# One group for linear attention's outputs, rests of x last, small products padded, a shorter Newton step: a hybrid decoder layer

## The chip, the cores and the metric

The kernel runs on one core of a Trainium2 chip. The metric is the device time of one execution in microseconds (us), median over several runs. A profile of one execution stands beside it, with its own time.

The core has five engines, each with its own queue of instructions: TensorE (PE; PEld is its load of the stationary operand), VectorE (DVE), ScalarE (ACT), GpSimd (POOL) and SyncE (SP), which here issues nearly all DMAs. An engine takes its instructions in the order in which they were written for it, and waits by semaphores.

## The reference, cut to what matters

One decoder layer for 512 prompt tokens and 8 running sequences of one new token each. One projection of x (1024 wide) gives the columns of two mixers and their gates:

```python
h = jnp.einsum('btd,de->bte', x, w_in)
qa, ka, va, za, ga, qb, kb, vb, gb = jnp.split(h, split_points, axis=-1)
log_a = log_sigmoid(einsum(za, w_alpha2) + b_alpha) / 16
o_a, s_new = gla_chunked(qa, ka, va, log_a, s0, chunk)      # gated linear attention, 4 heads
o_a = o_a * lax.rsqrt(jnp.mean(jnp.square(o_a), -1, keepdims=True) + RMS_EPS) * gla_norm_g
o_b = dilated_attention(qb, k_all, v_all, q_idx, rel_bias)  # 8 heads, three window patterns
mix = jnp.concatenate([o_a * silu(ga), o_b * silu(gb)], axis=-1)
y = jnp.einsum('bte,ed->btd', mix, w_out)
x_new = layer_norm(DEEPNORM_ALPHA * x + y, ln_g, ln_b)
```

In a chunk of linear attention an output is the product of the chunk's own attention matrix with the values, plus the product of the decayed queries with the state before the chunk. For the running sequences the 1024 past keys and values are read from a cache.

## The kernel before, in words

**A planner writes the order.** Every step is a generator (`dense`, `gla_out`, `sample_softmax`, ...) that yields one operation at a time, or waits for a mark (`At`), a buffer (`Need`), several at once (`Pair`) or a batch that stays together (`Batch`). `Plan.run` (L300) takes, again and again, the operation that can start soonest by estimated costs (L95 to L123), ties by the step's priority, and writes it to its engine. So all five queues are fixed when the program is built, from estimates, and another cost or another buffer can move operations on any engine. All operations are written at L359; a reader finds them by the names of their tiles. Among the estimates is one for a change of TensorE's tile form: `SWITCH = 230.0` ns.

**Buffers** are slots by tag (L58): among them `t2=3`, `pr=4`, `t1=6`, `sv=4`. PSUM has eight banks: three `d`, three `s`, two `t`.

**Products in full precision.** A float32 operand is split in a high part, cut by ScalarE's copy to a shorter format, and a rest, which VectorE subtracts (`split`, L412). A product is three: high x high, high x rest, rest x high. Weights (hi, lo) and x (xh, xl) both go that way. Other small products are taken in plain float32, which the trace shows as two passes each.

**The stages.** `first_loads` (L536) loads x in eight slices of 128 features and the weights of ka in between, `zw`, the constants `cf` and the table `rel_bias`, copied to 64 rows (`rb_raw`, L554, two DMAs); then `weight_loads` runs through the other weight groups, two raw buffers at a time. `first_splits` (L563) splits x slice by slice, the first slice in two column ranges (`TS`: the 256 first tokens with the 8 samples, and the 256 last), the others whole, and marks `xs` each. `dense` (L681) starts with warm-up products, then takes ka: for each slice k and column range u, for both halves i of ka's features, the three products in a row (L691 to L696). It waits for x's rest before any of a slice's products. Then come za, qa, qb, kb, vb, gb, va and ga, and the output projection: `out_first` (L1473) takes the features of tokens 0 to 255 and the samples, `out_unit` (L1461) the last 256 tokens.

**Linear attention** (`gla_levels`, `gla_diagonal`, `gla_state`, `gla_queries`) builds the attention matrices `att0`, `att1`, the states `st_all` after each of four token tiles, and the decayed queries. `gla_out(u)` (L961) then takes the outputs of two token tiles: a batch of 8 products att x values with 128 rows and of 4 or 8 products queries x state with 64 rows each, into two `s` banks. It is started twice, u = 0 after the first state, u = 1 after the third. `gla_head` (L981) evacuates them and normalises; `mix_a` (L1393) multiplies with the gate.

**The running sequences.** `sample_queries` (L1211) loads for each of them the keys (`past`) and its query, copied to all partitions (`qbc`, a `t2` buffer); GpSimd multiplies, VectorE adds up into `lt`. `sample_softmax` (L1231) sums in one bank, `ps_sl`, a table product (66 rows, 64 columns), the new key's logits (32 rows, 64 columns) and the transposed `lt` (128 rows, 64 columns); softmax, `psd_s` to DRAM, and a product `ps_pn` with 64 rows. `sample_values`, `sample_gla` follow; `mix_sample_a` and `mix_sample_b` make their part of the output projection's input.

**The ends.** `residual_sample` (L1525) normalises the samples' output on 64 rows, with two sums over features by products of 64 rows and 64 columns (`ps_ms`, `ps_vs`). `norm(t)` (L1560) normalises a token tile: `rsqrt` (L388) with `between` set takes the logarithm, the exponential and then a Newton step on ScalarE in four instructions (square, times x, times -0.5 plus 1.5, times the estimate), while VectorE centres the tile; then VectorE scales and adds, and the tile is stored.

## Time and profile before

| | |
|---|---|
| median of 3 runs | 287.93 us (287.79 to 289.35) |
| the profiled execution, its own time | 288.67 us |
| its span | 286.8 us |
| instructions | 6896 |
| TensorE's clock as granted, mean | 0.994 |
| HBM read, written | 45.17 MB, 6.03 MB |

The span runs from the first instruction of the program to the last; the execution's own time holds a little more around it. Busy shares of the engines are averages over stages that differ, so a part of the change is read in its own stage. In a row of the timeline the columns are the start in us, the time that the row's instructions span, engine, line, operation, output tile and its inputs, TensorE's tile form (rows * columns) where it has one, shape, count, and in brackets the idle time before it with what ended it. Matmuls overlap: the distance from one start to the next is what a product costs, not its own duration.

### The profile page before, as it was taken

The numbers are of one execution on the slowest core, as the hardware profiler recorded it, in microseconds if no ns is written. First come the engines' busy times: TensorE is split into PE (matmuls) and PEld (weight loads), VectorE is DVE, ScalarE is ACT, GpSimd is POOL, SyncE is SP. The second block draws the span as 40 slices with busy tenths as digits, with TensorE's granted clock in tenths as the row PEclk, the third lists the DMA queues.
The fourth block names the chain that finished last, engine by engine and source line by source line (L and its number), as shares of the span: only waits on it lengthen the run. The fifth ranks groups of instructions, "written<-read, shape, count | busy, mean of one in ns | idle before, by whom it ended". The sixth has DMA issues, their size and how long they took to land.

```text
span 286.8 us, 6896 instructions
## 1 busy us (share of the span) xinstructions
PE 275.0 (96%) x2636; PEld 259.5 (90%) x2636; DVE 225.7 (79%) x547; ACT 167.5 (58%) x478; POOL 55.9 (19%) x74
## 2 busy tenths in 40 slices
PE   8999999999999998999999999999999999999990
PEld 5899999998989998899989999999999999997880
DVE  3846897999889968988889997864888995339745
ACT  5757664554567777566869867526689774113201
POOL 4000001000782444401604444540000000000000
PEclk9999999999999999999999999999999999999997
DMA  7966522225866797648998987559754788741211
GB/s 209 269 191 195 147 75 75 75 78 167 296 201 222 196 287 230 175 130 243 274 201 188 239 227 219 149 149 228 221 95 148 230 297 252 111 151 73 78 75 73
DMA packets 58936, 51.18 MB, mean 178 GB/s; under 512 B 12555, under 2 KB 50197, under 8 KB 58903
## 3 DMA queue, kind: packets, MB, share of 16 engines
q1 hardware_dynamic: 58794, 50.66, 63.2%
q8 instruction: 21, 0.34, 0.5%
q14 instruction: 13, 0.10, 0.1%
q10 hardware_dynamic: 108, 0.07, 0.1%
HBM read 45.17 MB, written 6.03 MB: 179 GB/s over the span
## 4 chain that ended last, share of the span: by engine, by line
PE 71%; DVE 13%; DMA 8%; ACT 5%; issue 2%; SPq 1%; DVEq 0%; ACTq 0%
PE ps_qb L359 8%; PE ps_yf L359 8%; PE ps_y L359 8%; PE ps_ga L359 6%; PE ps_kb L359 4%; PE ps_qa L359 4%; PE ps_gb L359 4%; PE ps_va L359 4%; PE ps_ka L359 4%; DMA raw_gb__2152<-in_w_in_dram 3%; DMA out_dram<-feat 3%; PE ps_pt L359 2%; PE ps_va_f L359 2%; PE ps_l L359 2%; PE ps_s L359 2%; PE ps_pv L359 2%
## 5 line engine op out<-in xcount | busy, mean ns | idle before, releaser
L359 POOL TENSOR_TENSOR vv<-vv,pb 128x256 f32<-128x256 f32 x32 | 26.1, 846 | 45.5 <-DMA pb<-psd_s 39.8
L359 POOL TENSOR_TENSOR past<-past,qbc 128x256 f32<-128x256 f32 x32 | 25.6, 831 | 43.4 <-DMA past<-in_ck_dram 36.0
L359 ACT ACTIVATE pr<-pr,ms 128x128 f32<-128x128 f32 (+3 forms) x49 | 26.1, 546 | 5.8 <-DVE ms L359 5.2
L359 PE MATMUL ps_pt<-cf,pr 128*128 128x128 f32 x80 | 14.1, 280 | 1.4 <-DVE pt L359 1.0
L359 DVE CUSTOM_DVE_ANT_0 pr<-ps_s,strip 128x128 f32<-128x128 f32 (+3 forms) x32 | 14.3, 476 | 0.0
L359 PE MATMUL ps_ka<-xx,hi_ka 128*128 128x264 f32 (+1 forms) x64 | 13.5, 307 | 0.3 <-DVE xx L359 0.3
L359 ACT ACTIVATE sg<-sg 128x264 f32<-128x264 f32 (+1 forms) x32 | 13.4, 419 | 0.2
L359 PEld LDWEIGHTS ps_ka<-xx,hi_ka 128*128 128x128 f32 x64 | 11.0, 205 | 1.2 <-DVE xx L359 0.8
L359 DVE TENSOR_TENSOR ptl<-ps_pt,pth 128x384 fp32r<-128x384 f32 (+1 forms) x16 | 9.8, 617 | 2.8 <-ACT pth L359 2.8
L359 PEld LDWEIGHTS ps_pt<-cf,pr 128*128 128x128 f32 x80 | 9.0, 140 | 3.3 <-DVE pt L359 1.6
L359 ACT ACTIVATE d<-d 128x512 f32<-128x512 f32 x13 | 7.8, 637 | 6.7 <-DVE d L359 6.7
L359 ACT COPY feat_y<-ps_yf 128x256 f32<-128x256 f32 x8 | 3.0, 371 | 12.7 <-PE ps_yf L359 12.7
L359 ACT ACTIVATE rstd<-mv 128x1 f32<-128x1 f32 x4 | 0.7, 199 | 15.9 <-DVE mv L359 15.9
L359 POOL MEMSET att<- 64x512 f32 x2 | 1.0, 523 | 44.5 <-DVE ks L359 44.5
L359 ACT CAST pth<-ps_pt 128x384 fp32r<-128x384 f32 (+1 forms) x16 | 8.4, 534 | 2.2 <-PE ps_pt L359 2.0
L359 DVE TENSOR_REDUCE o_pv<-vv 128x4 f32<-128x1024 f32 x8 | 9.7, 1212 | 0.0
L359 DVE TENSOR_REDUCE lt<-past 128x16 f32<-128x1024 f32 x8 | 9.6, 1199 | 0.0
L359 PE MATMUL ps_ka<-xx,lo_ka 128*128 128x264 f32 (+1 forms) x32 | 9.4, 295 | 0.0
L359 DVE TENSOR_TENSOR obT<-ps_pv,pvl 64x256 f32<-64x256 f32 x16 | 6.6, 415 | 3.5 <-ACT pvl L359 3.3
L359 DVE TENSOR_TENSOR xx<-x_raw,xx 128x520 fp32r<-128x520 f32 (+2 forms) x9 | 5.8, 640 | 4.6 <-ACT xx L359 4.6
L359 ACT COPY pvl<-ps_pv 64x256 f32<-64x256 f32 x16 | 5.5, 370 | 6.1 <-PE ps_pv L359 5.3
L359 DVE TENSOR_TENSOR d<-b 128x1024 f32<-128x1024 f32 x7 | 8.5, 1218 | 0.0
(535 smaller groups left out, 1092.4 us busy)
## 6 DMA issues: line engine op xcount, KB each, us to landing
past<-in_ck_dram SPq DMA_DIRECT2D x8, 512.0 KB
vv<-in_cv_dram SPq DMA_DIRECT2D x8, 512.0 KB
pb<-psd_s SPq DMA_DIRECT2D x16, 256.0 KB
qbc<-qsd SPq DMA_DIRECT2D x8, 256.0 KB
strip<-tabr SPq DMA_DIRECT2D x8, 256.0 KB
y<-in_xp_dram SPq DMA_DIRECT2D x4, 512.0 KB
x_raw<-in_xT_dram SPq DMA_DIRECT2D x7, 260.0 KB
out_dram<-y SPq DMA_DIRECT2D x3, 512.0 KB
```

What stands on the lines that cost most here:

```text
L359: getattr(eng.eng, op.fn)(*op.args, **op.kw)
```

## The change

It has four parts.

1. `gla_out` runs once, for all four token tiles: four banks from `s` and `t` together, 16 products att x values, then the 12 with the states. It waits for the third state.
2. In ka's products a slice's four products with x's high part go first, the two with x's rest last. Slices 1 and 2 are split in the two column ranges as well, as slice 0 was.
3. Products with fewer than 128 rows or columns are padded to full size: those of `ps_sl`, `ps_pn`, `ps_ms` and `ps_vs`. The table is loaded twice as wide, the constants `sel` and `avg` on 128 rows; `l32`, `pn_r` and `sums` are cleared first; `lt` gets a third part, where `q_s` and `k_s` now lie. The raw copy of the second table (`cts_raw`) takes a `t2` buffer instead of a `pr` one.
4. In `rsqrt` with `between`, the variance is made -0.5 (x + eps), the logarithm takes it times -2, and one instruction does what "times x" and "times -0.5 plus 1.5" did.

```diff
+N_HALF = 3
...
         if between:
 
+            yield V.tensor_scalar(x, x, eps, -0.5, op0=ALU.add, op1=ALU.mult)
+            yield S.activation(o, x, AF.Ln, scale=-2.0)
+            yield S.activation(o, o, AF.Exp, scale=-0.5)
             add(between, 5)
             yield S.activation(t, o, AF.Square)
-            yield S.mul(t, t, x)
-            yield S.activation(t, t, AF.Copy, scale=-0.5, bias=1.5)
+            yield S.activation(t, t, AF.Copy, scale=x, bias=1.5)
             yield S.mul(o, o, t)
...
-        B["rb_raw"] = yield Need("t1", "rb_raw", [64, NB, HB])
+        B["rb_raw"] = yield Need("t1", "rb_raw", [64, 2 * NB, HB])
...
-                yield from split(xraw[a // 2][:, a % 2, c], xh[a][:, c], xl[a][:, c])
-                mark("xs")
+                for c in (c,) if b or a >= N_HALF else TS:
+                    yield from split(xraw[a // 2][:, a % 2, c], xh[a][:, c], xl[a][:, c])
+                    mark("xs")
...
-                for i in range(2):
-                    yield from three(pk[i, u][:, :TW[u]], k, halves(k, u, groups[f"ka{i}"]))
+                for last in (False, True):
+                    for i in range(2):
+                        pairs = halves(k, u, groups[f"ka{i}"])
+                        for j in (1,) if last else (0, 2):
+                            yield T.matmul(pk[i, u][:, :TW[u]], *pairs[j], start=k == 0 and j == 0, stop=k == KT - 1 and last)
...
-    def gla_out(u):
+    def gla_out():
 
-        yield At("st", 2 * u + 1)
+        yield At("st", 3)
...
-        ps = yield Pair(*(bank("s", f"ps_oa{u}{h2}") for h2 in range(2)))
+        banks = yield Pair(*(bank(("s", "t"), f"ps_oa{u}{h2}") for u in range(2) for h2 in range(2)))
...
-        sel = yield Need("t1", "sel", [64, C_AV - C_E2])
-        yield D.dma_start(sel, c_f[:64, C_E2:C_AV])
+        sel = yield Need("t1", "sel", [P, C_AV - C_E2])
+        yield D.dma_start(sel, c_f[:, C_E2:C_AV])
...
-        raw = yield Need("pr", "cts_raw", [66, T_W - T_D])
+        raw = yield Need("t2", "cts_raw", [66, T_W - T_D])
...
-        yield T.matmul(ps[:64, :258], rb.rearrange("p b h -> p (b h)"), cts, start=True, stop=False, skip_group_check=True)
-        yield T.matmul(ps[:64, 256:257], l32, one[:32], start=False, stop=False, skip_group_check=True)
+        yield T.matmul(ps[:, :258], rb.rearrange("p b h -> p (b h)"), cts, start=True, stop=False, skip_group_check=True)
+        yield T.matmul(ps[:, 256:257], l32, one, start=False, stop=False, skip_group_check=True)
         for k in range(2):
-            yield T.matmul(ps[:64, k * P:k * P + P], lt[:, k, :], ident, start=False, stop=k == 1, skip_group_check=True)
+            yield T.matmul(ps[:, k * P:k * P + P], lt[:, k:k + 2, :].rearrange("p a b -> p (a b)"), ident, start=False, stop=k == 1, skip_group_check=True)
...
-        yield T.matmul(ps[:64, 0:1], avg, sums[:, 0:1], start=True, stop=True)
+        yield T.matmul(ps[:, 0:1], avg, sums[:, 0:1], start=True, stop=True)
```

More of the change, by code (lines that the diff above doesn't have):

```diff
@@ L921, in gla_state @@
         st = B["st"] = yield Need("g", "st_all", [P, TT, 2, P])
-        plan.share(st, 3)
+        plan.share(st, 2)
         kv = yield Pair(*(bank("s", f"ps_kv{cc}") for cc in range(2)))
@@ L971, in gla_out @@
                         B["st"][h2 * 64:h2 * 64 + 64, 2 * u + j - 1, m, :], start=False, stop=j + m == 2, skip_group_check=True)
-               for j in range(2) for m in range(2) for h2 in range(2) if u + j]
+               for u in range(2) for j in range(2) for m in range(2) for h2 in range(2) if u + j]
         yield mm
         free(qd, B["st"], *att)
-        plan.share(va, 2)
-        for h2 in range(2):
-            plan.share(ps[h2], 2)
-        for j in range(2):
-            add(gla_head(u, j, ps, po), 26 + u + j / 2)
+        for u in range(2):
+            plan.share(B[f"va{u}"], 2)
+            ps = banks[2 * u:2 * u + 2]
+            for h2 in range(2):
+                plan.share(ps[h2], 2)
+            for j in range(2):
+                add(gla_head(u, j, ps, {k[1:]: x for k, x in po.items() if k[0] == u}), 26 + u + j / 2)
```

69 lines of the change are left out of this document (36 added, 33 removed).

## The prediction

> **What bounds the kernel now.** I read the page's engine totals first, then the busy time by stage, then TensorE's timeline where the change edits it. Every instruction sits on helper line L359, so rows are found by tile.
>
> ```profile
> PE 275.0 (96%) x2636; PEld 259.5 (90%) x2636; DVE 225.7 (79%) x547; ACT 167.5 (58%) x478; POOL 55.9 (19%) x74
> ...
> 8.00:18.00 10.00, 10.00 (x82) 9.79 (x82) 6.53 (x12) 6.14 (x10) 0.00 (x0) 1.00 0.97 272
> ...
> 112.00:124.00 12.00, 10.65 (x83) 9.18 (x82) 11.69 (x30) 8.33 (x24) 6.01 (x7) 1.00 0.56 165
> ...
> 268.00:279.30 11.30, 11.27 (x73) 10.02 (x71) 6.63 (x12) 1.40 (x6) 0.00 (x0) 1.00 0.13 51
> ```
>
> The columns of a stage are its length, then busy time of TensorE, its weight loads, VectorE, ScalarE, GpSimd, the granted clock, the DMA share and GB/s. TensorE is busy 275.0 of 286.80 us, and full in the last product stage. What it no longer has to do, or no longer waits for, comes off the end unless something later holds it. The stage from 112 to 124 us is the exception: TensorE is busy 10.65 of 12.00 and VectorE 11.69, so there VectorE sets the pace. The 82 products from 8 to 18 us give 10.00/82 = 0.12 us per product.
>
> The profiled execution took 288.67 us, its span 286.80, so 1.87 us lie around the span. The median of the three runs is 287.93 (287.79 to 289.35), 0.74 below the profiled one. I sum the terms against 288.67 and subtract the sum from the median.
>
> **First products.** In each of the eight slices of x a product takes the high part, and another the rest, which ScalarE and then VectorE must make first.
>
> ```profile
> 6.39 0.62 ACT L359 CAST xx<-x_raw 128x520 fp32r<-128x520 f32 x1 [0.76 <-DMA x_raw<-in_xT_dram]
> 7.05 0.70 DVE L359 TENSOR_TENSOR xx<-x_raw,xx 128x520 fp32r<-128x520 f32 x1 [0.96 <-ACT xx L359]
> ...
> 7.07 0.39 PE L359 MATMUL ps_ka<-xx,hi_ka 128*128 128x264 f32 x1
> 7.80 0.39 PE L359 MATMUL ps_ka<-xx,hi_ka 128*128 128x264 f32 x1 [0.34 <-DVE xx L359]
> ...
> 9.52 0.19 PEld L359 LDWEIGHTS ps_ka<-xx,hi_ka 128*128 128x128 f32 x1 [0.21 <-DVE xx L359]
> ```
>
> The second slice's first product starts at 7.07, its second at 7.80, after the rest ends at 7.75: 0.73 less one pitch of 0.12 is 0.61 us lost. The third slice loses 0.21. After the change four products go ahead of the two that take the rest, so the rest is needed at 7.07 + 4 x 0.12 = 7.55. Halves cost at least half and at most all of a whole: the first half's rest is ready between 6.39 + 0.31 + 0.35 = 7.05 and 6.39 + 0.62 + 0.70 = 7.71. I take it as ready. TensorE then ends the first products 0.61 + 0.21 = 0.82 us sooner at best, and 0.66 if the half costs all of a whole.
>
> But that is not yet time won. The next group's weights come through a queue that the change lengthens:
>
> ```profile
> 236.08 13.93 SPq L359 DMA_DIRECT2D out_dram<-kw  x16
> ...
> 10.03 1.65 SPq L359 DMA_DIRECT2D rb_raw<-in_rel_bias_dram  x2
> ...
> 13.27 0.38 SPq L359 DMA_DIRECT2D raw_qa__174<-in_w_in_dram  x1
> ...
> 17.11 1.05 ACT L359 CAST hi_qa__264<-raw_qa__174 128x1024 fp32r<-128x1024 f32 x1 [1.81 <-DMA raw_qa__174<-in_w_in_dram]
> ...
> 18.27 1.15 DVE L359 TENSOR_TENSOR lo_qa__265<-raw_qa__174,hi_qa__264 128x1024 fp32r<-128x1024 f32 x1
> ...
> 20.44 0.41 PE L359 MATMUL ps_qa<-xx,hi_qa__264 128*128 128x264 f32 x2
> ```
>
> The two rb_raw transfers go from 256 pieces each to 512, and SyncE already spends 1.65 us on issuing them, ahead of raw_qa. ScalarE waits 1.81 us for raw_qa, so a later issue moves hi_qa and lo_qa. With 0.82 us gained TensorE reaches qa at 19.62 and wants lo_qa two products later, at 19.86; lo_qa ends at 18.27 + 1.15 = 19.42. The cover is 0.44 us. The issue grows by nothing up to all of 1.65: at that end lo_qa ends at 21.07, where before it was wanted at 20.68, and 0.39 is lost. The nearest row is the keys' store, whose 16 transfers also have 512 pieces each (32 rows of 16) and take 13.93/16 = 0.87 us: two are 1.74, 0.09 more than now, which the cover takes. If the cover is gone, each further us of issue costs one. I take the middle of 0.66 and 0.82, so 0.74 us gained, bounds -0.39 to 0.82. The extra instructions of the halves on ScalarE and VectorE are in the 0.66.
>
> **One output group.** Two groups run, each 16 passes of full size and then passes on 64 rows.
>
> ```profile
> 200.82 1.95 PE L359 MATMUL ps_oa<-va,att 128*128 128x128 f32 x16
> ...
> 202.69 0.71 PE L359 MATMUL ps_oa<-st_all,qa 64*128 64x128 f32 x8
> 203.34 0.39 PE L359 MATMUL ps_ga<-xx,lo_ga__2975 128*128 128x264 f32 x1
> ...
> 206.07 1.95 PE L359 MATMUL ps_oa<-va,att 128*128 128x128 f32 x16
> ...
> 207.95 1.16 PE L359 MATMUL ps_oa<-st_all,qa 64*128 64x128 f32 x16
> ...
> 209.04 0.51 PE L359 MATMUL ps_ga<-xx,hi_ga__2974 128*128 128x256 f32 x2
> ```
>
> Eight 64-row passes more take (209.04 - 207.95) - (203.34 - 202.69) = 0.44 us, so eight cost 0.44 and leaving costs 0.65 - 0.44 = 0.21. Entering costs 1.87 less 16 passes at 0.11 (0.44/4 for a pair is the same pitch), 0.11. One of two entries and exits falls away: 0.32, and the first product after the exit, which is slow too, gives up to another 0.12. I take 0.40, bounds 0.32 to 0.44. The price is that the first group's results come with the second's, and four of the five s and t banks are held. The group waits for the last state; gate products, which lie behind no wait of it, fill TensorE until then, as they did between 203.34 and 206.07.
>
> **Padded products.** Products on 64 rows or columns become full size.
>
> ```profile
> 259.66 0.39 PE L359 MATMUL ps_y<-lo_wo__3465,mha 128*128 128x512 f32 x1
> 259.98 0.27 PE L359 MATMUL ps_ms<-sums_s,avg 64*64 64x1 f32 x2
> 260.18 0.50 PE L359 MATMUL ps_y<-hi_wo__3464,mla 128*128 128x512 f32 x1
> 260.52 0.40 PE L359 MATMUL ps_y<-hi_wo__3525,mha 128*128 128x512 f32 x1
> ...
> 247.42 0.38 PE L359 MATMUL ps_yt<-cf,feat_y 128*128 128x128 f32 x2
> 247.56 0.37 PE L359 MATMUL ps_yf<-mhb,lo_wo__3690 128*128 128x264 f32 x1
> 247.76 0.28 PE L359 MATMUL ps_yf<-mlb,hi_wo__3689 128*128 128x264 f32 x1
> ...
> 123.47 0.28 PE L359 MATMUL ps_sl<-cts,rb 66*64 66x258 f32 x1
> 123.68 0.27 PE L359 MATMUL ps_sl<-cf,l 32*64 32x1 f32 x2
> 123.88 0.65 PE L359 MATMUL ps_sl<-cf,lt 128*64 128x128 f32 x4
> 124.46 0.50 PE L359 MATMUL ps_pv<-pt,vhl 128*128 128x256 f32 x2
> ```
>
> From 259.66 to 260.52 TensorE does two 512-wide products and the two passes of ps_ms in 0.86 us. Two such products take about 4 x 0.12 = 0.48 (a 512-wide one moves twice a 256-wide one's columns), so ps_ms costs 0.38. The nearest full-size row is ps_yt: two passes begin at 247.42, and the second product after them at 247.76, 0.34 less one product's 0.12: 0.22. Each of the two sums saves 0.16, both 0.32 (bounds 0 to 0.5). The logits take 124.46 - 123.47 = 0.99 now; full size they are one product at 0.12 and six passes at 0.11, 0.78. That saves 0.21, bounds 0 to 0.33. The small product ps_pn follows score products in their own 64-row form now and so pays no entry of its own; padded it costs up to 0.22: I take 0.09 lost.
>
> The Trainium skill, TensorEngine Tiling (Array Packing), section Performance Considerations, speaks against this: a contraction of at most 64 rows should use row tiling. By it the sum would be 0.44 smaller. The 16 row-tiled passes of ps_oa here agree, running eight in 0.44 us, but ps_ms has no partner to share the array with.
>
> The padding adds clears on VectorE: 128x128, 128x32 and 128x2.
>
> ```profile
> 18.17 0.17 DVE L359 MEMSET tsb<- 8x128 f32 x1
> ```
>
> In the stage paced by VectorE the first costs about this, 0.17; the others are covered (VectorE has 12.00 - 11.69 = 0.31 us idle in that stage). Without cover the three cost 0.51.
>
> **Newton step.** Only the last token tile's is on the path.
>
> ```profile
> 281.41 0.29 ACT L359 ACTIVATE newton<-newton,mv 128x1 f32<-128x1 f32 x1
> 281.74 0.20 ACT L359 ACTIVATE newton<-newton 128x1 f32<-128x1 f32 x1
> 281.97 0.29 ACT L359 ACTIVATE rstd<-rstd,newton 128x1 f32<-128x1 f32 x1
> 282.30 1.41 DVE L359 SCALAR_TENSOR_TENSOR y<-y,rstd,beta 128x512 f32<-128x512 f32 x2 [0.31 <-ACT rstd L359]
> ```
>
> The product and the plain step become one with an operand for its scale, at the product's price: the start-to-start of the plain step, 0.23, falls away. VectorE is free from 282.30 - 0.31 = 281.99, so up to 0.31 can be used. Gain 0.23, bounds 0.2 to 0.31.
>
> **Sum.** 0.74 + 0.40 + 0.32 + 0.21 - 0.09 - 0.17 + 0.23 = 1.64. Profiled, 288.67 - 1.64 = 287.03; by the median 287.93 - 1.64 = 286.29, so 286.3. All low bounds give -0.39 + 0.32 + 0 + 0 - 0.22 - 0.51 + 0.2 = -0.60, all high ones 0.82 + 0.44 + 0.5 + 0.33 + 0.31 = 2.40: 288.5 and 285.5.
>
> **The rivals.**
>
> First: the gain of the first products is lost in the stage that VectorE paces. For it: 1.35 us of TensorE's 12.00 are idle there from 112 to 124. Against: VectorE has 3.47 us idle from 8 to 18 and its work then comes sooner too. The sum loses 0.74: 287.0.
>
> Second: the order is redrawn. A program with planned costs writes every engine's order, and new costs move it everywhere. Idle time of TensorE like the 1.35 us may go or double elsewhere. Gone, it gives 286.3 - 1.35 = 284.9; doubled, 287.6. Nothing in the profile says which.
>
> Third, slower: the t2 buffers. The second table's raw copy moves from the pr buffers to the three of t2, which the broadcast query rows need.
>
> ```profile
> 132.90 9.72 DMA raw_gb__2152<-in_w_in_dram
> ...
> 232.65 0.18 DVE L359 TENSOR_TENSOR mla<-ga_s,mha 128x32 fp32r<-128x32 f32 x1
> ...
> 238.03 0.28 PE L359 MATMUL ps_yf<-mha,hi_wo__3464 128*128 128x264 f32 x1
> ```
>
> If the last query row has to wait for that copy, then the samples' logits, softmax, values and state all come later. Their end is the row at 232.83, wanted at 238.03: 5.20 us of slack. A copy as slow as the transfer that the chain of waits shows, 9.72, overruns it by 4.5, giving 290.8. It decides from a delay of 6.8 us (slack and sum). Against: only queries later than the copy can wait, and one is left.
>
> Fourth: padding saves nothing, as a full-size product may hold TensorE for as long as the small one and its change of form: the sum loses 0.32 + 0.21 - 0.09 = 0.44, giving 286.7. The rule of the Trainium skill on row tiling, above, would lead here.
>
> **How the numbers follow.** About 0.5%, 1.44 us, is what a measurement of this kernel can tell from no change: faster means below 286.49. The forecast gets 0.50: 0.36 below that line, because the sum lies past it, and 0.14 within, because it is past by only 0.2. The first rival gets 0.18, within. The second gets 0.16 on its good side, faster, and 0.08 on its bad side, within. The third gets 0.05, slower, the fourth 0.03, within. Faster 0.52, same 0.43, slower 0.05. The range runs from 284.9, the second rival's good side, to 288.3, just inside all low bounds; it leaves out the third rival and the tail beyond the second.
>
> **What would show it.** Right: no wait at the second slice; ps_ka done about 0.8 us sooner; qa's first product near 19.8; ps_oa as one group with one entry and exit; ps_ms, ps_vs and ps_sl at 128*128 with about 0.11 us per pass; five ScalarE steps instead of six before the last scaling. Wrong: hi_qa cast after 18.2, TensorE idle for 2.7 us (twice the 1.35) in the stage that holds the logits' product, or the samples' last row ending after 238.

## The result, and the profile after

The changed kernel took 291.48 us (median of six runs, 290.86 to 291.92), the kernel before 288.62 on the same occasions (six runs, 287.79 to 289.35). The ratio is 1.0083 with a 95% interval of 1.0054 to 1.0112: slower by 0.8%, where the forecast was 286.3, with a range from 284.9 to 288.3. Here and below the ratio is that of the fast executions; the quotient of the two medians, 1.0099 here, is another number, but lies inside the interval each time. The profiled execution of the changed kernel took 290.86 us, its span 289.1.

In the lines below every instruction of the changed kernel sits on line L360, the same helper one line further down. First the engine totals and the busy time by stage; the columns are those of the prediction. Of the stages from 160 to 172, 196 to 208 and 208 to 220 us the prediction showed nothing, so those of the kernel before come first.

```profile
160.00:172.00 12.00, 11.96 (x99) 11.18 (x99) 11.74 (x30) 8.70 (x24) 5.67 (x8) 1.00 0.86 229
196.00:208.00 12.00, 12.00 (x120) 11.32 (x119) 9.60 (x33) 7.94 (x34) 0.00 (x0) 1.00 0.83 225
208.00:220.00 12.00, 12.00 (x108) 11.88 (x108) 10.25 (x36) 11.06 (x39) 0.00 (x0) 1.00 0.55 139
```

And the changed kernel:

```profile
PE 274.5 (95%) x2636; PEld 260.0 (90%) x2636; DVE 227.4 (79%) x556; ACT 167.3 (58%) x472; POOL 55.3 (19%) x74
...
112.00:124.00 12.00, 10.93 (x86) 9.64 (x86) 11.49 (x31) 8.67 (x25) 6.23 (x8) 1.00 0.60 180
160.00:172.00 12.00, 10.85 (x89) 9.89 (x88) 11.94 (x28) 8.44 (x23) 6.11 (x8) 1.00 0.82 216
196.00:208.00 12.00, 12.00 (x129) 11.45 (x128) 6.30 (x18) 6.49 (x18) 0.00 (x0) 1.00 0.60 163
208.00:220.00 12.00, 10.86 (x90) 10.66 (x90) 11.30 (x49) 10.94 (x52) 0.00 (x0) 1.00 0.72 180
```

TensorE is busy for 0.5 us less than before (274.5 against 275.0), as the change meant it to be, and yet the span is 2.3 us longer. So the loss is in waits. Two stages hold most of it: TensorE is idle for 1.15 us from 160 to 172 (0.04 before) and for 1.14 us from 208 to 220 (none before). In the stage ahead of that, 196 to 208, it is VectorE that does less: 6.30 us of work in place of 9.60. What it did not do there stands in the next stage, 11.30 in place of 10.25.

The first group of weights after the first products. The lines are of SyncE's queue, ScalarE, VectorE and TensorE, in the order of their starts:

```profile
10.28 2.21 SPq L360 DMA_DIRECT2D rb_raw<-in_rel_bias_dram  x2
...
14.04 0.38 SPq L360 DMA_DIRECT2D raw_qa__179<-in_w_in_dram  x1
...
18.83 1.05 ACT L360 CAST hi_qa__270<-raw_qa__179 128x1024 fp32r<-128x1024 f32 x1 [3.15 <-DMA raw_qa__179<-in_w_in_dram]
...
20.04 1.15 DVE L360 TENSOR_TENSOR lo_qa__271<-raw_qa__179,hi_qa__270 128x1024 fp32r<-128x1024 f32 x1
...
20.35 0.40 PE L360 MATMUL ps_qa<-xx,hi_qa__270 128*128 128x264 f32 x2
...
21.24 0.40 PE L360 MATMUL ps_qa<-xx,lo_qa__271 128*128 128x264 f32 x1 [0.48 <-DVE lo_qa__271 L360]
```

The two rb_raw transfers take 2.21 us to issue, 0.56 more than before. From the issue of raw_qa to the cast that waits for it pass 18.83 - 14.04 = 4.79 us, before 17.11 - 13.27 = 3.84: the weights do not only start later (14.04 against 13.27, 0.77), they also take 0.95 longer to land. lo_qa is ready at 21.19, and TensorE waits for it.

The output group: TensorE first, then VectorE, then SyncE's queue.

```profile
202.27 3.73 PE L360 MATMUL ps_oa<-va,att 128*128 128x128 f32 x32
205.94 1.61 PE L360 MATMUL ps_oa<-st_all,qa 64*128 64x128 f32 x24
207.47 0.50 PE L360 MATMUL ps_ga<-xx,hi_ga__2978 128*128 128x256 f32 x2
...
202.51 0.87 DVE L360 SCALAR_TENSOR_TENSOR s<-v,ka_s,s 128x128 f32<-128x128 f32 x3
206.68 0.35 DVE L360 SCALAR_TENSOR_TENSOR oa<-va,dg,ps_oa 128x128 f32<-128x128 f32 x1 [3.30 <-PE ps_oa L360]
...
209.47 0.57 SPq L360 DMA_DIRECT2D s<-in_state_dram  x1
```

and the same two engines in the kernel before:

```profile
201.55 2.18 DVE L359 SCALAR_TENSOR_TENSOR s<-v,ka_s,s 128x128 f32<-128x128 f32 x8
203.66 1.63 DVE L359 SCALAR_TENSOR_TENSOR oa<-va,dg,ps_oa 128x128 f32<-128x128 f32 x6
...
204.20 0.57 SPq L359 DMA_DIRECT2D s<-in_state_dram  x1
```

The group takes TensorE from 202.27 to 207.47, 5.20 us; the two groups before took 2.52 + 2.97 = 5.49. That gain is there. But VectorE carries out its instructions in the order in which they were written. Before, it did all eight products of the first half of the samples' states (s) and then found the first group's result ready. Now it does three of them, comes to the group's first result, and stands for 3.30 us, with five products behind it that need nothing of the group. The second half of the states, whose load waits for those products, is asked for at 209.47 in place of 204.20. Two TensorE waits follow (the last line is VectorE's):

```profile
217.49 0.52 PE L360 MATMUL ps_ga<-xx,hi_ga__3127 128*128 128x264 f32 x2 [1.14 <-DVE ga L360]
...
232.50 0.33 PE L360 MATMUL ps_ort<-cf,o_r 128*128 128x128 f32 x1 [0.58 <-DVE ga L360]
...
231.70 1.40 DVE L360 SCALAR_TENSOR_TENSOR ga<-ps_oat,gn,ga 128x512 f32<-128x512 f32 x2
```

At 216 VectorE is behind with emptying the gate products' banks. At 232 TensorE comes to the turning of the samples' rows o_r (ps_ort). VectorE finishes these rows at 231.78, before at 227.66; but by the row the wait lasts until VectorE's next pass, the first of the two ga passes from 231.70. It ends at 232.44 and empties one of the two `t` banks, which ps_oat holds and ps_ort needs. The output products queue behind the turning.

The small products, and the end of the last token tile:

```profile
122.88 0.28 PE L360 MATMUL ps_vb<-hi_vb__1822,xx 128*128 128x256 f32 x1
...
123.36 0.28 PE L360 MATMUL ps_sl<-cts,rb 66*128 66x258 f32 x1
...
124.07 0.60 PE L360 MATMUL ps_pv<-pt,vhl 128*128 128x256 f32 x4
...
262.51 0.40 PE L360 MATMUL ps_y<-lo_wo__3483,mha 128*128 128x512 f32 x1
262.74 0.28 PE L360 MATMUL ps_ms<-sums_s,avg 128*128 128x1 f32 x2
262.88 0.48 PE L360 MATMUL ps_y<-hi_wo__3482,mla 128*128 128x512 f32 x1
263.20 0.39 PE L360 MATMUL ps_y<-hi_wo__3527,mha 128*128 128x512 f32 x1
...
281.49 0.28 PE L360 MATMUL ps_y<-hi_wo__3797,mla 128*128 128x256 f32 x1
...
284.57 1.41 DVE L360 SCALAR_TENSOR_TENSOR y<-y,rstd,beta 128x512 f32<-128x512 f32 x2
```

From 262.51 to 263.20 TensorE needs 0.69 us for what took 0.86 before (259.66 to 260.52): the full-size sum saves 0.17. The logits take 124.07 - 123.36 = 0.71 in place of 0.99. From TensorE's last start to VectorE's last scaling pass 3.08 us; before, that product started at 278.98 and the scaling at 282.30, 3.32. These parts do what they were priced at.

Last, the wait in the stage from 160 to 172:

```profile
168.41 0.28 PE L360 MATMUL ps_gb<-xx,lo_gb__2268 128*128 128x256 f32 x1
169.73 0.51 PE L360 MATMUL ps_va_f<-xx,hi_va__2463 128*128 128x264 f32 x2 [1.04 <-DVE ms L360]
```

The next unit waits for VectorE's row maximum of a score tile (ms), whose reading frees the bank. VectorE is busy for 11.94 of the 12 us there.

### The profile page after: what moved, and what is told of

It is laid out like the page before. It is cut to its first block, busy times and chain, and to the rows that moved or that the text cites. A ratio compares the mean times of both kernels' runs of the same rounds, so it can differ in the third digit from the quotient of the medians.

```text
span 289.1 us, 6890 instructions
## 1 busy us (share of the span) xinstructions
PE 274.5 (95%) x2636; PEld 260.0 (90%) x2636; DVE 227.4 (79%) x556; ACT 167.3 (58%) x472; POOL 55.3 (19%) x74
## 4 chain that ended last, share of the span: by engine, by line
PE 55%; DVE 23%; DMA 10%; ACT 7%; issue 2%; SPq 1%; DVEq 0%; ACTq 0%
PE ps_qb L360 8%; PE ps_yf L360 8%; PE ps_y L360 8%; PE ps_kb L360 7%; PE ps_va_f L360 4%; PE ps_qa L360 4%; PE ps_va L360 4%; DVE pr L360 3%; DMA out_dram<-feat 3%; DMA x_raw<-in_xT_dram 3%; PE ps_l L360 2%; DMA ct_raw<-in_c_t_dram 2%; PE ps_s L360 2%; DMA raw_va__2507<-in_w_in_dram 2%; PE ps_oa L360 1%
## 5 line engine op out<-in xcount | busy, mean ns | idle before, releaser
L360 POOL TENSOR_TENSOR vv<-vv,pb 128x256 f32<-128x256 f32 x32 | 25.7, 832 | 46.5 <-DMA pb<-psd_s 38.8
L360 POOL TENSOR_TENSOR past<-past,qbc 128x256 f32<-128x256 f32 x32 | 25.3, 824 | 43.3 <-DMA past<-in_ck_dram 36.9
L360 ACT ACTIVATE pr<-pr,ms 128x128 f32<-128x128 f32 (+3 forms) x48 | 25.3, 541 | 4.0 <-DVE ms L360 3.5
L360 DVE CUSTOM_DVE_ANT_0 pr<-ps_s,strip 128x128 f32<-128x128 f32 (+3 forms) x32 | 14.2, 475 | 0.0
L360 PE MATMUL ps_pt<-cf,pr 128*128 128x128 f32 x80 | 13.4, 277 | 0.6 <-DVE pt L360 0.5
L360 PE MATMUL ps_ka<-xx,hi_ka 128*128 128x264 f32 (+1 forms) x64 | 13.3, 304 | 0.3 <-ACT xx L360 0.3
L360 ACT ACTIVATE sg<-sg 128x264 f32<-128x264 f32 (+1 forms) x32 | 13.3, 417 | 0.2
L360 ACT ACTIVATE d<-d 128x512 f32<-128x512 f32 x13 | 7.8, 637 | 6.7 <-DVE d L360 6.7
L360 PEld LDWEIGHTS ps_ka<-xx,hi_ka 128*128 128x128 f32 x64 | 10.9, 204 | 0.8 <-ACT xx L360 0.5
L360 ACT COPY feat_y<-ps_yf 128x256 f32<-128x256 f32 x8 | 3.0, 372 | 12.9 <-PE ps_yf L360 12.9
L360 PEld LDWEIGHTS ps_pt<-cf,pr 128*128 128x128 f32 x80 | 9.1, 140 | 1.4 <-DVE pt L360 0.7
L360 DVE TENSOR_TENSOR ptl<-ps_pt,pth 128x384 fp32r<-128x384 f32 (+1 forms) x16 | 9.5, 611 | 0.9 <-ACT pth L360 0.9
L360 DVE TENSOR_REDUCE o_pv<-vv 128x4 f32<-128x1024 f32 x8 | 9.7, 1212 | 0.7 <-POOL vv L360 0.6
L360 ACT COPY pvl<-ps_pv 64x256 f32<-64x256 f32 x16 | 5.9, 370 | 7.1 <-PE ps_pv L360 6.1
L360 DVE TENSOR_TENSOR obT<-ps_pv,pvl 64x256 f32<-64x256 f32 x16 | 6.6, 414 | 4.1 <-ACT pvl L360 3.9
L360 ACT ACTIVATE rstd<-mv 128x1 f32<-128x1 f32 x4 | 0.7, 200 | 15.7 <-DVE mv L360 15.7
L360 POOL MEMSET att<- 64x512 f32 x2 | 1.0, 524 | 45.1 <-DVE ks L360 45.1
L360 DVE TENSOR_TENSOR xx<-x_raw,xx 128x520 fp32r<-128x520 f32 (+2 forms) x11 | 5.9, 552 | 4.8 <-ACT xx L360 4.8
L360 ACT CAST pth<-ps_pt 128x384 fp32r<-128x384 f32 (+1 forms) x16 | 8.4, 532 | 2.1 <-PE ps_pt L360 1.9
L360 DVE TENSOR_REDUCE lt<-past 128x16 f32<-128x1024 f32 x8 | 9.6, 1200 | 0.0
L360 PE MATMUL ps_ka<-xx,lo_ka 128*128 128x264 f32 (+1 forms) x32 | 8.9, 298 | 0.0
L360 DVE TENSOR_SCALAR pr<-pr,ms 128x384 f32<-128x384 f32 (+3 forms) x16 | 8.5, 537 | 0.2
```

The costliest lines, as they stand in the source:

```text
L360: getattr(eng.eng, op.fn)(*op.args, **op.kw)
```

## The experiments

The first theory was that the merged group is the main loss, by VectorE's wait. The first rival was the table of twice the width, whose transfers delay the weights of qa. The second was that any edit redraws the planned order and moves some wait. All times in one table, beside the kernel before on the same chip; the last three columns are from each kernel's profiled execution, starts of TensorE's products in us:

| kernel | median us | before us | ratio (95% interval) | first ps_qa | first ps_kv to first ps_yf | last ps_y |
|---|---|---|---|---|---|---|
| before | 288.62 | | | 20.44 | 31.39 | 278.98 |
| changed | 291.48 | 288.62 | 1.0083 (1.0054, 1.0112) | 20.35 | 33.18 | 281.49 |
| e1_group_undone | 289.73 | 288.97 | 1.0018 (0.9987, 1.0049) | 20.54 | 31.37 | 279.72 |
| e2_order_undone | 291.81 | 288.97 | 1.0103 (1.0073, 1.0133) | 20.78 | 33.17 | 281.07 |
| e3_table_undone | 290.24 | 288.97 | 1.0031 (1.0001, 1.0061) | 20.14 | 32.78 | 280.87 |
| e4_group_alone | 291.51 | 288.97 | 1.0092 (1.0057, 1.0127) | 20.65 | 33.18 | 281.35 |
| e5_products_first | 290.48 | 289.78 | 1.0031 (0.9999, 1.0063) | 21.04 | 30.38 | 280.79 |
| e6_order_sums_newton | 288.29 | 289.78 | 0.9957 (0.9920, 0.9994) | 19.57 | 31.39 | 279.95 |
| e7_table_alone | 291.64 | 289.78 | 1.0073 (1.0043, 1.0103) | 21.05 | 30.94 | 282.77 |
| e8_order_alone | 289.23 | 289.78 | 0.9993 (0.9959, 1.0028) | 19.66 | 31.39 | 278.71 |
| e9_table_on_chip | 287.98 | 289.75 | 0.9959 (0.9927, 0.9992) | 20.31 | 31.37 | 278.15 |
| e10_pool_later | 295.81 | 289.75 | 1.0232 (1.0191, 1.0274) | | | |
| e11_before_pool_later | 297.22 | 289.75 | 1.0275 (1.0227, 1.0324) | | | |
| e12_on_chip_pool_later | 300.35 | 289.75 | 1.0383 (1.0329, 1.0437) | | | |
| e13_group_on_chip | 290.11 | 289.59 | 1.0041 (1.0009, 1.0074) | 19.80 | 33.16 | 280.13 |
| e14_both_mended | 288.16 | 289.59 | 0.9957 (0.9931, 0.9984) | 20.86 | 30.38 | 279.49 |
| e15_halves_in_turn | 290.07 | 289.59 | 1.0006 (0.9974, 1.0039) | | | |
| e16_turn_later | 288.61 | 289.44 | 0.9982 (0.9951, 1.0014) | 19.76 | 30.38 | 280.09 |

One thing has to be known for reading single executions: TensorE's first waits, for x and the first weights, differ between them by up to about 1 us in the sum, whatever the kernel (compare ps_qa of e9, e13, e14 and e16, whose code is the same that far: 19.76 to 20.86). So the early rows are read by their distances, and small differences of the total by the ratios. The last three columns are left out for four kernels: in e10 to e12 the products ps_og come behind the first ps_yf, and e15's profiled execution took 292.28 us, the longest of its twelve. In e3, e5, e7, e14 and e16 other products stand between ps_kv and ps_yf than before (in e5, e7, e14 and e16 ps_ort comes after).

**Parts undone and alone.** In e1_group_undone the two groups are apart again:

```
-        add(gla_out(), 26)
+            add(gla_out(u), 26 + u)
```

> The changed kernel with its two output groups apart again, as before; the rest of the change stays. Theory (the merged group is the main loss: VectorE idle 3.30 us ahead of the group's results, then TensorE's waits of 1.42 us at 216 and 0.86 us at 231.6): both waits go, 291.48 - 2.28 = 289.2, and 288.6 to 289.9. Rival 1 (the table of twice the width, whose issue delays the weights of qa by 1 to 2 us, is the loss): no change by this, 291.0 to 291.8. Rival 2 (any edit redraws the planned order and moves some wait by about 1.3 us, as the new one at 168.4): any time from 290.2 to 292.8, with the waits in other places.

In e2_order_undone the first products stand in their old order and x's slices are whole:

```
-                for c in (c,) if b or a >= N_HALF else TS:
-                    yield from split(xraw[a // 2][:, a % 2, c], xh[a][:, c], xl[a][:, c])
-                    mark("xs")
+                yield from split(xraw[a // 2][:, a % 2, c], xh[a][:, c], xl[a][:, c])
+                mark("xs")
```

> The changed kernel with the first products in their old order and x's slices whole; the rest stays. Theory (group): the 0.47 us that the last ps_ka started sooner is not worth anything, as qa waits for its weights then; 291.5, and 291.2 to 291.9. Rival 1 (table): the same, as the weights of qa come no sooner. Rival 2 (order redrawn): 290.2 to 292.8.

In e3_table_undone the table and the logits' products have their old width:

```
-    rb = cst("rb", [66, 2 * NB, HB], F32R)
+    rb = cst("rb", [66, NB, HB], F32R)
...
-        yield T.matmul(ps[:, :258], rb.rearrange("p b h -> p (b h)"), cts, start=True, stop=False, skip_group_check=True)
+        yield T.matmul(ps[:64, :258], rb.rearrange("p b h -> p (b h)"), cts, start=True, stop=False, skip_group_check=True)
```

> The changed kernel with the bias table at 64 columns and the logits' products at 64 columns again; sums, ps_pn, groups, order and Newton step stay changed. Theory (group): lo_qa is ready about 1.2 us sooner, but 96 us into the run only 0.23 us of that delay was left, and the 0.2 us of the padded logits is lost again: 291.4, and 290.9 to 291.9. Rival 1 (table): the weights of qa come 0.8 to 1.8 us sooner and this comes off the end, 289.7 to 290.7. Rival 2 (order redrawn): 290.2 to 292.8.

And e4_group_alone is the kernel before with the merged group only (the e1 edit the other way, on the kernel before).

> The kernel before with only the two output groups merged. Theory (group): 288.62 + 2.28 - 0.29 (TensorE's own gain on the group) = 290.6, and 290.0 to 291.2, with VectorE idle about 3 us ahead of the group's results. Rival 1 (table): TensorE's own gain remains, 288.3, and 288.0 to 288.7. Rival 2 (order redrawn): 287.3 to 290.0, with no link between VectorE's idle time and the end.

e1 came out as the theory said (289.73), and e4 a little above it (291.51, expected up to 291.2): without the group 0.65 points of the 0.83% are gone, and the group alone makes the kernel before slower by 0.92%. The column from ps_kv to ps_yf is the clearest proof, since it is a difference within one execution. In nine kernels that stretch holds the same 304 passes of TensorE: it takes 31.37 to 31.39 us in the five with the groups apart (before, e1, e6, e8, e9) and 33.16 to 33.18 in the four with the merged one (changed, e2, e4, e13), whatever else differs between them. e2 was as expected too: 0.2% above the changed kernel, which the intervals don't tell from nothing, so there is no sign that the order by itself does harm. e3 was a miss: I had given the table nearly nothing at the end, and undoing it took off half a per cent, as the first rival had it (290.24, in its 289.7 to 290.7; 1.0031 of 288.62 is 289.5, a little below). So the group was not the only loss.

**The table.** e7_table_alone is the kernel before with the wide table and the padded logits, e8_order_alone the kernel before with the first products' order, and e6_order_sums_newton has that order, the two padded sums and the Newton step, but neither table nor group.

> The kernel before with only the bias table of twice the width and the logits' products padded to full size. Theory: SyncE issues 0.56 us longer, lo_qa comes 1 to 1.7 us later, TensorE waits for it by 0.3 to 0.9 us, and of that about half is left at 200 us: 289.0, and 288.5 to 289.6, with ps_sl taking 0.7 us in place of 0.99. Rival 1 (the table is a loss of its own size at the end): 289.7 to 290.5. Rival 2 (the logits' padding outweighs it): 288.4 or less.

> The kernel before with only the first products' order and x's first slices in halves. Theory (VectorE's stage from 112 to 172 us takes the gain): the last ps_ka 0.4 to 0.7 us sooner, qa's products as much, and the first ps_va_f near 168 again: 288.5, and 288.0 to 289.0. Rival (the gain reaches the end): 287.9, and 287.6 to 288.0, all later rows 0.7 us sooner.

> The kernel before with the first products' order, the padded ps_ms and ps_vs and the shorter Newton step; no merged group, bias table and logits as before. Theory (what the first products gain is used up again between 112 and 172 us, where VectorE is busy for over 11.4 of 12 us): only 0.32 + 0.23 of the sums and the Newton step is left of it, 288.1, and 287.5 to 288.6. Rival (without the wide table the first products' gain reaches the end): 288.62 - 0.74 - 0.55 = 287.3, and 286.8 to 287.5.

e7 lost 0.73%, more than the theory had and a little more than the first rival (1.0073 of 288.62 is 290.7, and its range ends at 290.5); e8 came out by the theory, and e6 (0.9957 of 288.62 is 287.4) by its rival; more on these two below. But e7's planned order differs from the one before in hundreds of places, so this alone doesn't say whether the transfers did it. e9_table_on_chip settles that. It is e1's kernel, order and all, except that the table is loaded at its old width and read twice by the two instructions that round it:

```
-        B["rb_raw"] = yield Need("t1", "rb_raw", [64, 2 * NB, HB])
+        B["rb_raw"] = yield Need("t1", "rb_raw", [64, NB, HB])
...
-        yield S.copy(rb[:64], raw)
+        rr = rb.rearrange("p (a b) h -> p a (b h)", a=2)
+        r2 = raw.rearrange("p b h -> p (b h)")[:, None, :].to_broadcast([64, 2, NB * HB])
+        yield S.copy(rr[:64], r2)
```

> The changed kernel with the output groups apart, and with the bias table loaded at its old width and doubled on the chip by the copy and the subtraction that were there already (their inputs read twice); every engine's order is that of the kernel with the groups apart, which came to 1.0018 of the time before. Theory (the table costs what its transfers cost: 0.56 us more of issue and the smaller pieces ahead of qa's weights): hi_qa and lo_qa come about 1.2 us sooner, no wait in the first products of qa, and at the end 0.3 to 1.2 us less: 288.4, and 287.8 to 288.9 (0.997 to 1.001 of before). Rival (the table alone lost 0.73% through the logits' products or another planned order): 289.1 as with the groups apart, and 288.9 to 289.6.

e1's queue and cast:

```profile
10.23 2.12 SPq L360 DMA_DIRECT2D rb_raw<-in_rel_bias_dram  x2
...
13.89 0.38 SPq L360 DMA_DIRECT2D raw_qa__179<-in_w_in_dram  x1
...
18.87 1.04 ACT L360 CAST hi_qa__270<-raw_qa__179 128x1024 fp32r<-128x1024 f32 x1 [3.49 <-DMA raw_qa__179<-in_w_in_dram]
```

and e9's:

```profile
10.65 1.31 SPq L360 DMA_DIRECT2D rb_raw<-in_rel_bias_dram  x2
...
13.57 0.38 SPq L360 DMA_DIRECT2D raw_qa__179<-in_w_in_dram  x1
...
17.51 1.05 ACT L360 CAST hi_qa__270<-raw_qa__179 128x1024 fp32r<-128x1024 f32 x1 [2.06 <-DMA raw_qa__179<-in_w_in_dram]
```

Issue to cast falls from 18.87 - 13.89 = 4.98 us to 17.51 - 13.57 = 3.94, the issue of the table from 2.12 to 1.31. The ratio falls from 1.0018 to 0.9959. With the order of every engine the same, the table's transfers are shown to be the cause, at about 0.6% by the ratios. All 18 profiled executions show the same two groups: with the wide table (changed, e1, e2, e5, e7) the issue takes 2.12 to 2.31 us and the cast follows raw_qa's issue after 4.79 to 5.40; with the old width (the other 13) it is 1.11 to 1.70 and 3.84 to 4.22. The delay also travels to the end. As the orders are the same, TensorE's starts can be subtracted product by product: e9 is 0.52 us later than e1 ahead of qa, 1.03 earlier behind qa's first products, and 1.57 earlier at the last product; e13 (below) is 0.18, 1.31 and 1.36 earlier than the changed kernel at the same places. The total came out even a little better than expected. This kernel, the whole change without merged group and wide load, is faster than the changed kernel, and by 0.4% (0.1 to 0.7) than the one before.

**Where the gain of the first products goes.** In e8 and e6 qa's first product starts at 19.66 and 19.57, 0.8 to 0.9 us sooner than before, 0.3% of the time. Single starts vary by as much, but over all traces the gain is there: from the first pass of ps_ka to the last 13.79 to 14.39 us (median 14.00) in the five with the old order, and 12.89 to 14.20 (median 13.28) in the 13 with the new one. e8's total is 0.9993 of before. e6's is 0.9957, of which the two sums and the Newton step explain 2 x 0.17 + 0.24 = 0.58 us, 0.2%. So the order brings 0.1 to 0.2% at the end, and the intervals tell that neither from nothing nor from all of it. In single executions one sees it being lost. e8 has the order of the kernel before on every engine, but for the first products themselves and the two more splits of x, so its lead can be followed. TensorE is 0.78 us ahead at the first ps_qa, 1.37 at the last ps_gb (166.66 against 168.03), 0.52 at the first ps_kv (197.93 against 198.45) and 0.27 at the last ps_y. In between it waits 0.61 us for ScalarE's feat at 172.04 and 0.45 for VectorE's ptl at 173.77, two waits that the kernel before does not have. In e6's profiled execution (289.32 us, one of its longer ones; the median is 288.29) the last of ps_gb is 1.79 us sooner than before (166.24 against 168.03); then come these rows, of VectorE, GpSimd and TensorE:

```profile
174.03 1.22 DVE L360 TENSOR_REDUCE o_pv<-vv 128x4 f32<-128x1024 f32 x1 [2.25 <-POOL vv L360]
...
170.94 3.05 POOL L360 TENSOR_TENSOR vv<-vv,pb 128x256 f32<-128x256 f32 x4 [6.38 <-DVE mlb L360]
...
175.92 0.41 PE L360 MATMUL ps_pt<-cf,pr 128*128 128x128 f32 x2 [2.07 <-DVE pr L360]
```

VectorE reaches the sum of a sample's values before GpSimd has multiplied them, and the scores behind it wait, and TensorE for those. I tried to take that wait away by telling the planner that GpSimd's results come later, in e6 (e10_pool_later), in the kernel before (e11_before_pool_later) and in e9 (e12_on_chip_pool_later):

```
-FROM_POOL = 2500.0
+FROM_POOL = 4000.0
```

> The kernel before with the first products' order, the padded sums and the Newton step, and with the planner told that GpSimd's results can be used 4.0 us after their end in place of 2.5 (one constant), so that VectorE's sums of the samples' values stand later in its queue. Theory (what the first products gain is lost where VectorE waits 2.25 us for GpSimd's product at 171.8, and TensorE behind it 2.35 us at 173.6): both waits go, 287.4 - 1.5 = 285.9, and 285.2 to 286.7. Rival (a redrawn order has such a wait in one place or the other): 287.0 to 288.8, with a wait of over 1 us elsewhere.

> The kernel before with that one planner constant changed and nothing else: what a redrawn order alone does. Theory: there is no wait for GpSimd to lose in it, 288.6, and 288.0 to 289.2. Rival (any redrawing moves the time by about as much as the parts of the change do): outside of 287.8 to 289.4.

> The changed kernel with the groups apart, the table doubled on the chip, and that planner constant changed. Theory: the sum of the parts that gain and none of the two that lose: 288.62 - 0.74 - 0.32 - 0.23 - 0.2 = 287.1 at the most, 286.2 if waits of VectorE for GpSimd go too; 285.6 to 287.4. Rival (redrawn order): 287.4 to 289.5.

All three missed: they are 2.3 to 3.8% slower than the kernel before. The rows that show it, in e11:

```profile
238.81 1.08 PE L359 MATMUL ps_og<-s,qx 128*32 128x128 f32 x32
242.61 0.30 PE L359 MATMUL ps_ort<-cf,o_r 128*128 128x128 f32 x1 [1.79 <-DVE o_r L359]
243.80 0.59 PE L359 MATMUL ps_yf<-mha,hi_wo__3451 128*128 128x264 f32 x1 [0.90 <-ACT mha L359]
```

In the kernel before, ps_og starts at 220.74. VectorE now comes late to the sums (the last one starts at 222.04, before at 189.75), the second half of the states is asked for at 223.23 (204.20), and everything of the samples follows. In e12 TensorE's granted clock is lower too, 0.969 to 0.975 against 0.985 to 0.995 in e9, so that its time is not waits alone. e11's rival held: one constant that redraws the order moves the time by 2.75%, more than any part of the change does. These runs show how little room the samples' chain has; that the wait for GpSimd in e6 is what ate the first products' gain in that execution stands in the rows, but no run took that wait away alone.

**Why the group loses.** Either VectorE's wait in order does it, or the four banks held and all heads' work at one time. e5_products_first is the changed kernel with one condition more: the heads' work may be written only after the eight products.

```
             for bb in range(4):
...
+            mark("half")
...
         oc, va = B[f"oa{u}"][:, j, :], B[f"va{u}"]
+        yield At("half")
```

> The changed kernel, in which the heads' work on the merged group's results may be written into the engines' orders only after all eight products of the first half of the samples' states, which need nothing of the group. Theory (the loss of the merged group is VectorE's idle 3.30 us, as the products stand behind the group's first result in its queue): five more products (1.4 us) lie in that idle time, the second load of the states goes at 205 to 206 in place of 209.47, and TensorE's waits at 216 and 231.6 (1.42 and 0.86 us) shrink by about 1.4 us in all: 290.1, and 289.4 to 290.7. Rival (all heads' work coming at once is the loss, whatever stands in front of it): 291.5, and 291.0 to 292.0.

e13_group_on_chip is the whole change with e9's table; e14_both_mended has both edits; and e15_halves_in_turn has e9's table and the merged batch with the first half's passes on the states ahead of the second half's passes:

```
-        mm += [T.matmul(po[u, h2, j, m], qd[h2 * 64:h2 * 64 + 64, m, (2 * u + j) * P:(2 * u + j) * P + P],
+        ms = [T.matmul(po[u, h2, j, m], qd[h2 * 64:h2 * 64 + 64, m, (2 * u + j) * P:(2 * u + j) * P + P],
...
+        mm[8:8] = ms[:4]
+        mm += ms[4:]
```

> The whole change, merged group and all, with only the bias table loaded at its old width and doubled on the chip; the engines' orders are those of the changed kernel. Theory (table and group cost by themselves, and the costs add): 291.48 - 1.75 = 289.7, and 289.1 to 290.3 (1.002 to 1.006 of before). Rival (qa's late weights are made good before the group is reached, so that the group alone sets the end): 291.0, and 290.7 to 291.6.

> The whole change with the table doubled on the chip, and the samples' first eight state products ahead of the heads' work in VectorE's queue. Theory (the group's loss is VectorE's wait in order; what is left of it uses up TensorE's own gain): 288.2, and 287.5 to 288.9, no better than the kernel with the groups apart and the table doubled on the chip, which came to 0.9959. Rival (once VectorE has work in front, TensorE's 0.3 to 0.4 us on the merged group reach the end): 287.0, and 286.5 to 287.3.

> The whole change with the table doubled on the chip, and the merged batch written so that the first token half's passes on the states follow its own full-size passes, ahead of the second half's: one more entry and exit of the 64-row form, four banks held as before. Theory (the loss comes from the first result's late time): the first result comes about 1.8 us sooner, VectorE's idle 3.30 us fall to about 1.5, 288.8, and 288.2 to 289.5. Rival (the four banks and the heads' work at one time are the loss): as with the table doubled alone and 0.2 to 0.3 us for the form, 289.9, and 289.5 to 290.6.

VectorE and the second load of the states in e14:

```profile
202.21 1.61 DVE L360 SCALAR_TENSOR_TENSOR s<-v,ka_s,s 128x128 f32<-128x128 f32 x5
...
204.19 0.87 DVE L360 SCALAR_TENSOR_TENSOR s<-v,ka_s,s 128x128 f32<-128x128 f32 x3
206.36 0.86 DVE L360 SCALAR_TENSOR_TENSOR oa<-va,dg,ps_oa 128x128 f32<-128x128 f32 x3 [1.30 <-PE ps_oa L360]
...
205.53 0.57 SPq L360 DMA_DIRECT2D s<-in_state_dram  x1
```

The same four banks, the same passes and the same 32 + 24 of them, and with eight products in front VectorE waits 1.30 us in place of 3.30 (3.29 in e13). The ratio falls from 1.0041 (e13) to 0.9957 (e14), and from 1.0083 to 1.0031 on the wide table (e5, by its theory): the merged group's loss is the wait in order, and not the four banks. The condition redraws little: against e13, 13 of TensorE's passes, one load of SyncE and some 30 instructions each of VectorE and ScalarE stand elsewhere, all behind the group's products. e13 lies 0.82% above e9, whose groups are apart (0.65% for the same step on the wide table), and 0.42% below the changed kernel (0.59% with the groups apart): within their intervals the two losses add. e15 came at it from the other side. Its 1.0006 is what the theory had (288.8 is 1.0006 of 288.62), but the interval reaches those of e13 and e14. VectorE's wait in its profiled execution, expected at about 1.5:

```profile
204.58 0.35 DVE L360 SCALAR_TENSOR_TENSOR oa<-va,dg,ps_oa 128x128 f32<-128x128 f32 x1 [1.50 <-PE ps_oa L360]
```

Yet e14 is no better than e9, as the theory had it: TensorE's own gain on the group doesn't reach the end. In e14 TensorE waits 0.89 us for o_r at ps_ort (start 232.61). e16_turn_later lets that turning be written only after three units' first halves:

```
+            mark("yf_half")
...
+        yield At("yf_half", 3)
         ps = yield bank("t", "ps_ort")
```

> The version with the table doubled on the chip and the products placed first, in which the turning of the samples' rows (ps_ort) may be written into TensorE's order only after the first halves of three output units: 26 products later. Theory (what is left of the merged group's loss is TensorE's wait of 1.17 us at 231.44 for o_r, in order): o_r is there at 232.5, ps_ort is reached near 233.6, the wait goes, and nobody waits for the samples' mixed rows before 237: 1.0 us off, 0.992 of before, and 0.989 to 0.9945. Rival (the output products then wait for the samples' rows, or the wait only moves): 0.9955 to 0.999.

The wait at ps_ort went, and a new one came 2.3 us ahead of it:

```profile
234.31 0.39 PE L360 MATMUL ps_yf<-mhb,hi_wo__3358 128*128 128x264 f32 x1 [0.68 <-DVE ga L360]
...
236.62 0.27 PE L360 MATMUL ps_ort<-cf,o_r 128*128 128x128 f32 x1
```

So the rival held: VectorE is behind with the gates (ga), and whoever comes first waits for it. Whether some order lets the group's 0.3 us through stays open.

## Why the prediction was wrong

**First products.** The step on the order itself held: qa's first product was forecast near 19.8 and starts at 19.66 with the order alone, and over all traces the first products take 0.72 us less by the medians above, where 0.74 was forecast. The step that failed is the price of the table: "The nearest row is the keys' store, whose 16 transfers also have 512 pieces each [...]: two are 1.74, 0.09 more than now, which the cover takes". The issue grew by 0.56, within the bound of 1.65 that I had written down but not believed; and the step counted the issue only. The weights behind the small pieces were issued 0.77 us later and took 0.95 longer to land, in all 18.83 - 17.11 = 1.72 for hi_qa, four times the cover of 0.44. "hi_qa cast after 18.2" was named as a sign of wrong, and it came. (The other two did not: TensorE is idle for 1.07 us from 112 to 124, and the samples' last row ends at 237.62.) At the end this costs 0.4 to 0.6% by the ratios (changed kernel against e13, where the intervals overlap, and e1 against e9), and 0.8 to 0.9% by the medians.

**The first rival**, that this gain is lost in a stage paced by VectorE, is not settled: the order alone gives 0.9993 (0.9959 to 1.0028), and a gain of 0.74 us, 0.26%, lies inside that interval as well. It looked for the loss from 112 to 124 us. In the profiled executions of e8 and e6 the lead is lost later, between 168 and 198 us, at the end of a stretch where VectorE was as full before (11.74 of 12 from 160 to 172) and behind it; the prediction does not read it.

**One output group.** TensorE's own gain was 0.29 (5.49 - 5.20), forecast 0.40 with bounds 0.32 to 0.44: below the low bound. The step that failed is the next one: "The price is that the first group's results come with the second's, and four of the five s and t banks are held." It has no number. What it says of TensorE is true, gate products fill it (12.00 of 12 from 196 to 208); but the results are taken by VectorE, whose queue the prediction does not read. The price was 1.79 us between ps_kv and ps_yf and 0.65 to 0.92% of the total (changed kernel against e1, e13 against e9, e4), the largest term of the whole change.

**Padded products.** Right in mechanism and near in size: 0.17 for the sum forecast at 0.16, 0.28 for the logits forecast at 0.21. ps_pn lost 0.13 (132.17 to 132.74 from the pass ahead of it to the product behind it, before 132.69 to 133.13), forecast 0.09. The fourth rival falls. The rule of the Trainium skill, TensorEngine Tiling (Array Packing), section Performance Considerations, that small contractions want row tiling, doesn't decide here: two passes with no partner are cheaper at full size by that 0.17 us.

**Newton step.** 3.32 - 3.08 = 0.24, forecast 0.23.

**The rest of the sum.** Without the group's 0.40 the forecast is 1.24 us, 0.43%. e9, which has the other parts and a table at the price that the forecast gave it, is 0.41% faster (0.08 to 0.73). That the two agree so closely is in part luck, since the 0.74 of the first products, the largest term, is not seen at the end of e8.

**The second and third rivals.** Most edits redraw the order (e2's and e8's don't), waits move with it (the 1.04 us ahead of 169.73 are new), and e11 shows that a redrawn order alone can cost more than any part of the change. So a single run with another order names no cause. But the two losses follow their parts through all these orders, and they come and go where the order is kept (e1 and e9, the changed kernel and e13) or differs only behind the group (e13 and e14), so redrawing is not the main cause. The third rival did not come: e9 has the raw copy in the t2 buffers too and is faster than before. The samples' last row does come late, at 237.62 in place of 232.83, but still ahead of the first product with mha, at 240.86. What makes the samples late is VectorE's queue.

**The chances.** Slower got 0.05, for one mechanism. A term whose price is a sentence without a number should have been a rival with a price. The range ended at 288.3, just inside all low bounds, so it held only the terms that had a number.

## What to carry to other kernels

When two batches become one, price the consumer's queue: list what stands on the engine that takes the results behind the first of them, and let independent work be written ahead of it. When a transfer is made of more small pieces, count what it does to the landing of the transfers behind it as well as the issue, and widen on the chip what can be widened there. And a gain at the start can be lost in any full stretch of another engine behind it: read each of them before counting it.

## What the runs showed of the hardware

Doubling the pieces of two small transfers, from 8 to 16 KB each, made the next big transfer land 0.95 to 1.04 us later, counted from its own issue (4.79 against 3.84, 4.98 against 3.94), beside 0.56 to 0.81 us of issue; the 18 profiled executions fall in two groups by the table's width (4.79 to 5.40 us and 3.84 to 4.22). The Trainium skill, DMA: Bandwidth & Descriptors, section Why small descriptors are slow (HBM only), gives each piece a fixed cost of its own beside its bytes; the direction agrees with these rows, which add what the transfer behind the pieces pays. VectorE took the merged group's first result at 206.68, though that tile's own last pass was one of the first 16 of the 32 that end at 206.00: the wait ended only after the passes on the states in the same half, which write the same banks, and with these moved ahead of the other half's 16 passes (e15) it fell from 3.30 to 1.50. Whether the chip or the program's own semaphores set this, no run tells.
